# Strassen's scheme for the gate and up projections of a two-layer diffusion trunk

## The chip, the cores and the metric

The kernel runs on the 8 cores of one Trainium2 chip. All cores run the same program: core i takes two of the 16 context sequences and one of the 8 latent grids. The metric is the device time of the slowest core in microseconds (us). Some executions were slower, with a lower granted clock on one die (cores 0 to 3, or cores 4 to 7).

## The reference, cut to what matters

Two layers, each a mixer and then a SwiGLU channel mixer; every sub-layer is normalised, scaled and shifted ("modulated"), and added through a gate.

```python
D_MODEL, D_FF = 1024, 2816
def swiglu(h, wg, wu, wd):
    return (jax.nn.silu(h @ wg) * (h @ wu)) @ wd

for i in range(DEPTH):                      # DEPTH = 2
    ...                                     # layer 0: pooling + attention; layer 1: chunk_gmlp
    ctx = ctx + cg1 * y_ctx
    lat = lat + lg1 * y_lat
    h_ctx = rms_norm(ctx, norm_ffn_g[i]) * (1 + csc2) + csh2
    h_lat = rms_norm(lat, norm_ffn_g[i]) * (1 + lsc2) + lsh2
    ctx = ctx + cg2 * swiglu(h_ctx, ffn_wg[i], ffn_wu[i], ffn_wd[i])
    lat = lat + lg2 * swiglu(h_lat, ffn_wg[i], ffn_wu[i], ffn_wd[i])
```

A core has three blocks of 512 tokens: block 0 is context, blocks 1 and 2 are latents. In this document "first mixer" and "second mixer" are the SwiGLUs of the two layers, and "gated mixer" is the spatial-gating MLP (`chunk_gmlp`) between them.

## The kernel before

Everything is fused into one program. The kernel holds a planner of its own: each part (a normalisation, a projection, a stream of loads) is a generator that yields what it needs next, and the planner picks, by assumed durations, what to emit next and on which engine. The order on each engine is thus **fixed when the kernel is built** (in the traces, all eight cores show the same order on each engine, wherever no matmul record is missing); at run time only the times move. `RANK` and `T` are tuned constants of this planner. Matrices are stored with features on the partitions; `h[b]` has 8 tiles of 128 features x 512 tokens.

The SwiGLU, 256 hidden columns per `k`, 11 values of `k` in four groups `GR`:

```python
GR = [(0, 3), (3, 6), (6, 9), (9, 11)]
def up(gi):
    k0, k1 = GR[gi]
    for b in blocks:
        ...
        for k in range(k0, k1):
            wg, wu = wts[("g", k)], wts[("u", k)]
            for jj in range(2):
                js = slice(jj * 128, (jj + 1) * 128)
                ...                                   # the context of layer 0 uses a tanh form
                pg, pu = P.bank(), P.bank()           # two PSUM banks
                P.mmg(pg[:], [(wg[:, kc, js], hb[:, kc, :]) for kc in range(8)])
                P.mmg(pu[:], [(wu[:, kc, js], hb[:, kc, :]) for kc in range(8)])
                sg = P.tmp(F32)
                P.act(sg[:], pg[:], AF.Silu)                                # ScalarE
                P.tt("dve", a[:, 2 * (k - k0) + jj, :], pu[:], sg[:], ALU.mult)  # VectorE
def down(gi): ...                                     # the group's part of (..) @ wd, added to x
for gi in range(len(GR)):
    yield from up(gi)
    if gi > 0:
        yield from down(gi - 1)
yield from down(len(GR) - 1)
```

The last step of every normalisation, per 128 features (`xb` is the residual x, `rs` the reciprocal root mean square), and the one rule by which the planner reckons with VectorE and GpSimd working at the same time:

```python
P.stt("dve", tmp[:], xb[:, kc, :], AA[..., kc, ...], rs[:], ALU.mult, ALU.mult)   # x * scale * rs
P.affine(hb[:, kc, :], tmp[:], 1.0, mscal(l, sh, kc, b))                          # + shift; ScalarE, VectorE or GpSimd
...
if e == "dve" and not self.single and not any("/" in r[0] for r in rr + wr):      # "/": a PSUM operand
    d = max([d] + [z - start + d - 100.0 for a, z in self.pool_ops if a <= start < z])
```

So a VectorE operation with no PSUM operand is assumed to wait for a GpSimd operation that is under way. `stt` sets `self.single`, so the scalar_tensor_tensor form is exempt, and GpSimd is never assumed to wait.

## Time and profile before

The time before is 1142.12 us (median of 4 runs, 1141.41 to 1144.61).

| before | value | read from |
|---|---|---|
| TensorE busy | 1095.9 us, 96% | page, part 1 |
| VectorE / ScalarE / GpSimd busy | 62% / 34% / 15% | page, part 1 |
| chain that ended last | 81% TensorE | page, part 4 |
| TensorE busy, 460 to 640 us (first mixer) | 179.89 of 180 us | table of stretches |
| TensorE busy, 640 to 860 us (gated mixer and its surroundings) | 212.46 of 220 us | table of stretches |

These are lines of the page of the kernel before (busy us, share of the span, instructions; then busy tenths in 40 slices; then the chain by engine):

```profile
span 1141.4 us, 16800 instructions; the slowest of 8 cores (1139.3 to 1141.4 us)
PE 1095.9 (96%) x6155; PEld 510.4 (45%) x6155; DVE 707.7 (62%) x1234; ACT 389.6 (34%) x613; POOL 168.3 (15%) x263
PE   5799899899999999999999999999999999999998
DVE  1196899635767986568676999858631143134257
POOL 6141102010101131020011023204000010000000
PE 81%; DVE 10%; DMA 4%; issue 2%; ACT 2%; POOL 1%; DVEq 0%; ACTq 0%; POOLq 0%
```

The same core by stretches; the columns are in the header line:

```profile
core 7: us, PE busy (x) PEld busy (x) DVE busy (x) ACT busy (x) POOL busy (x), PEclk, DMA share, GB/s
220.00:380.00 160.00, 158.84 (x1421) 84.32 (x1420) 96.49 (x178) 114.40 (x120) 18.45 (x35) 1.00 0.82 172
460.00:640.00 180.00, 179.89 (x834) 81.43 (x833) 129.69 (x216) 25.95 (x41) 18.16 (x31) 1.00 0.78 157
640.00:860.00 220.00, 212.46 (x1048) 97.77 (x1047) 164.24 (x317) 84.75 (x166) 49.27 (x52) 1.00 0.29 49
860.00:1178.00 318.00, 278.26 (x1290) 125.82 (x1287) 105.30 (x144) 28.66 (x48) 7.38 (x14) 1.00 0.22 47
```

The reader is to see a TensorE without slack from about 240 us on, VectorE at 72% beside it in the first mixer (129.69 of 180), and a GpSimd that does little.

### The profile page before, as it was taken

How to read it: one execution, taken by the hardware profiler on the slowest of the kernel's cores; microseconds unless marked ns; L12 is line 12 of the kernel's file. 1: busy time of each engine (PE TensorE's matmuls, PEld its weight loads, DVE VectorE, ACT ScalarE, POOL GpSimd, SP SyncE). 2: the span in 40 equal slices, each digit the busy share in tenths (PEclk: the TensorE clock that was granted, in tenths of full speed). 3: DMA queues.
4: the chain of work that ended last, by engine and by line, in shares of the span. 5: the costliest groups of instructions: out<-in, count | busy, mean ns of one | idle time of the engine just before them, and what ended most of it. 6: DMA issues, size and time to landing. Idle time of an engine off the chain costs nothing.

```text
span 1141.4 us, 16800 instructions; the slowest of 8 cores (1139.3 to 1141.4 us)
## 1 busy us (share of the span) xinstructions
PE 1095.9 (96%) x6155; PEld 510.4 (45%) x6155; DVE 707.7 (62%) x1234; ACT 389.6 (34%) x613; POOL 168.3 (15%) x263
## 2 busy tenths in 40 slices
PE   5799899899999999999999999999999999999998
PEld 2344443454555444444444444444444444444443
DVE  1196899635767986568676999858631143134257
ACT  2155756778776231130101173342311101100100
POOL 6141102010101131020011023204000010000000
PEclk7699799799999999999999999999999999999999
DMA  9998837495997589865689600040942182030006
GB/s 177 170 254 147 138 99 128 76 161 121 235 217 179 124 131 171 178 116 105 157 177 194 146 1 1 1 74 9 161 71 37 25 142 37 1 56 1 1 1 221
DMA packets 38750, 126.74 MB, mean 111 GB/s; under 512 B 4832, under 2 KB 6752, under 8 KB 38672
## 3 DMA queue, kind: packets, MB, share of 16 engines
q0 software_dynamic: 25520, 91.41, 46.4%
q1 hardware_dynamic: 13152, 34.27, 9.3%
q8 instruction: 52, 0.85, 0.3%
q14 instruction: 26, 0.21, 0.1%
HBM read 194.91 MB, written 6.88 MB: 177 GB/s over the span
## 4 chain that ended last, share of the span: by engine, by line
PE 81%; DVE 10%; DMA 4%; issue 2%; ACT 2%; POOL 1%; DVEq 0%; ACTq 0%; POOLq 0%
PE pp L521 81%; DMA adaw_121<-ada_w 3%; DVE adaj_2991 L581 1%; DMA adaw_1322<-ada_w 1%; DVE tf_86 L573 0%; DVE tf_87 L561 0%; DVE tf_88 L573 0%; DVE tf_85 L573 0%; DVE tf_84 L573 0%; DVE tf_87 L573 0%; ACT L557 0%; DVE kT_2310 L617 0%; DVE tf_83 L573 0%; ACT tf_84 L557 0%; DVE qT_1673 L617 0%
## 5 line engine op out<-in xcount | busy, mean ns | idle before, releaser
L557 ACT ACTIVATE tf_87<-pp 128x512 f32<-128x512 f32 x25 | 14.9, 596 | 125.8 <-PE pp L521 115.3
L557 ACT ACTIVATE tf_83<-pp 128x512 f32<-128x512 f32 x22 | 13.1, 597 | 92.7 <-PE pp L521 92.7
L557 ACT ACTIVATE tf_85<-pp 128x512 f32<-128x512 f32 x23 | 13.7, 597 | 58.0 <-PE pp L521 44.0
L557 ACT ACTIVATE tf_86<-pp 128x512 f32<-128x512 f32 x26 | 15.5, 597 | 51.3 <-PE pp L521 51.2
L557 ACT ACTIVATE tf_84<-pp 128x512 f32<-128x512 f32 x21 | 12.5, 597 | 48.8 <-PE pp L521 48.7
L557 ACT ACTIVATE tf_88<-pp 128x512 f32<-128x512 f32 x21 | 12.5, 596 | 47.4 <-PE pp L521 47.4
L557 ACT ACT_TABLE_LOAD x17 | 21.8, 1283 | 8.6 <-PE pp L521 7.4
L561 DVE TENSOR_TENSOR mod_47<-pp,vecs_43 128x4 f32<-128x4 f32 x24 | 3.7, 159 | 29.8 <-PE pp L521 29.7
L521 PE MATMUL pp<-ones_46 128*128 128x512 bf16 x50 | 18.2, 518 | 1.5 <-DVE frac_54 L588 1.5
L573 DVE SCALAR_TENSOR_TENSOR x_3568<-pp,mod_47,x_3568 128x512 f32<-128x512 f32 x20 | 15.0, 750 | 7.2 <-PE pp L521 6.8
L573 DVE SCALAR_TENSOR_TENSOR x_4671<-pp,mod_47,x_4671 128x512 f32<-128x512 f32 x20 | 14.8, 747 | 6.3 <-PE pp L521 6.1
L573 DVE SCALAR_TENSOR_TENSOR x_4673<-pp,mod_47,x_4673 128x512 f32<-128x512 f32 x20 | 14.8, 747 | 5.8 <-PE pp L521 5.5
L573 DVE SCALAR_TENSOR_TENSOR x_4668<-pp,mod_47,x_4668 128x512 f32<-128x512 f32 x20 | 14.8, 747 | 5.0 <-PE pp L521 4.8
L573 DVE SCALAR_TENSOR_TENSOR x_3572<-pp,mod_47,x_3572 128x512 f32<-128x512 f32 x20 | 14.8, 748 | 4.6 <-PE pp L521 4.3
L573 DVE SCALAR_TENSOR_TENSOR x_3577<-pp,mod_47,x_3577 128x512 f32<-128x512 f32 x20 | 14.6, 746 | 4.1 <-PE pp L521 3.9
L573 DVE SCALAR_TENSOR_TENSOR x_3574<-pp,mod_47,x_3574 128x512 f32<-128x512 f32 x20 | 14.7, 747 | 3.8 <-PE pp L521 3.5
L573 DVE SCALAR_TENSOR_TENSOR x_4666<-pp,mod_47,x_4666 128x512 f32<-128x512 f32 x20 | 14.8, 747 | 3.6 <-PE pp L521 3.3
L573 DVE SCALAR_TENSOR_TENSOR x_1793<-pp,mod_47,x_1793 128x512 f32<-128x512 f32 x12 | 9.0, 748 | 3.5 <-PE pp L521 3.3
L573 DVE SCALAR_TENSOR_TENSOR x_1799<-pp,mod_47,x_1799 128x512 f32<-128x512 f32 x12 | 9.0, 747 | 3.5 <-PE pp L521 3.3
L573 DVE SCALAR_TENSOR_TENSOR x_1790<-pp,mod_47,x_1790 128x512 f32<-128x512 f32 x12 | 8.9, 749 | 3.5 <-PE pp L521 3.3
L573 DVE SCALAR_TENSOR_TENSOR x_1795<-pp,mod_47,x_1795 128x512 f32<-128x512 f32 x12 | 8.9, 747 | 3.5 <-PE pp L521 3.3
L557 ACT ACTIVATE tf_86<-x_3568 128x512 f32<-128x512 f32 x2 | 1.3, 630 | 28.6 <-DVE x_3568 L573 28.6
(2108 smaller groups left out, 2991.7 us busy)
## 6 DMA issues: line engine op xcount, KB each, us to landing
w_uq_142<-w_uq POOLq DMA_DIRECT2D x1, 576.0 KB, 55.4
x_93<-x_in POOLq DMA_DIRECT2D x1, 512.0 KB, 6.6
x_95<-x_in POOLq DMA_DIRECT2D x1, 512.0 KB, 7.3
x_97<-x_in POOLq DMA_DIRECT2D x1, 512.0 KB, 9.2
x_99<-x_in POOLq DMA_DIRECT2D x1, 512.0 KB, 10.0
adaw_107<-ada_w POOLq DMA_DIRECT2D x1, 512.0 KB, 20.0
adaw_109<-ada_w POOLq DMA_DIRECT2D x1, 512.0 KB, 22.6
adaw_111<-ada_w POOLq DMA_DIRECT2D x1, 512.0 KB, 24.7
```

Of the source, the lines that this page charges most:

```text
L521: ins = self.op("pe", lambda g: g.matmul(out, lhsT, rhs, start=start, stop=stop, **kw), [lhsT, rhs], [out], (c, 190), inc=inc)
L557: return self.op("act", lambda g: g.activation(out=out, in_=in_, func=func, bias=bias, scale=scale, **kw), reads, writes, d)
L561: return self.op(e, lambda g: g.tensor_tensor(out=out, in0=in0, in1=in1, op=op), [in0, in1], [out], self._d(e, out, [in0, in1], "tt"))
L573: ins = self.op(e, lambda g: g.scalar_tensor_tensor(out=out, in0=in0, scalar=sc, in1=in1, op0=op0, op1=op1), reads, [out], self._d(e, out, ...
L581: return self.op(e, lambda g: g.scalar_tensor_tensor(out=out, in0=in0, scalar=1.0, in1=in1, op0=ALU.mult, op1=ALU.mult, accum_out=acc), [i ...
```

## The change

Intent: gate and up tile of 128 hidden columns, times two halves of tokens, times two halves of the 1024 features, make a 2x2 block product of 8 block products. Strassen's scheme needs seven, so TensorE does 28 matmuls for 32, and sums of weights, sums of tokens and sums of results go to the other engines. It is used for latents in both layers (the halves are blocks 1 and 2) and for the context in the second (the halves are 256 tokens each). The first layer's context part stays plain.

```diff
+            def quad(p, k, jj, a):                    # cut: names of the blocks, yields
+                P.grow(v(E), P1)
+                P.copy(v(x1), v(E), engs=cp)          # cp = ("act",)
+                P.grow(v(F), P2)
+                P.tt("dve", v(x1), v(F), v(x1), ALU.add)
+                P.grow(v(C), P5)
+                P.copy(v(x3), v(C), engs=cp)
+                P.grow(v(E), P6, False)
+                P.copy(v(x2), v(E), engs=cp)
+                P.grow(v(C), P3, False)
+                P.tt("dve", v(x2), v(C), v(x2), ALU.add)
+                P.grow(v(E), P7, False)
+                P.copy(v(x4), v(E), engs=cp)
+                P.add2(v(x3), v(x3), v(x4), ALU.add)  # add2, mul: VectorE or GpSimd, as the planner picks
+                P.act(v(x3), v(x3), AF.Silu)
+                P.grow(v(E), P4, False)
+                P.act(v(x4), v(E), AF.Silu)
+                P.mul(a[b2][:, j, o2:o2 + n], v(x2), v(x3))
+                P.mul(a[b1][:, j, o1:o1 + n], v(x1), v(x4))
+            def wsum(k):                              # per 256 hidden columns
+                P.add2(s1[:], a21, a22, ALU.add)
+                P.add2(a21, a11, a21, ALU.subtract)   # in place: wg's tile is used up
+                P.add2(s2[:], s1[:], a11, ALU.subtract)
+                P.add2(s4[:], a12, s2[:], ALU.subtract)
+            def token_sums(p):                        # once per mixer and pair of halves, all on VectorE
+                yield U("dve", cond=has(...))         # both halves' normalised blocks must be there
+                for out, p_, q_ in ((T1[:], b12, b11), (T2[:], b22, T1[:]), (b12, b22, b12), (T4[:], b21, T2[:])):
+                    P.tt("dve", out, p_, q_, ALU.subtract)
```

With it came three things that are not the scheme: a new path in all normalisations,

```diff
-                P.stt("dve", tmp[:], xb[:, kc, :], AA[:, l, w, kc, ci:ci + 1], rs[:], ALU.mult, ALU.mult)
-                P.affine(hb[:, kc, :], tmp[:], 1.0, mscal(l, sh, kc, b))
+                xk, ak = xb[:, kc, :], AA[:, l, w, kc, ci:ci + 1]
+                if P.pick2(("dve", "pool"), "tt", tmp[:], [xk, rs[:]]) == "pool":
+                    P.tt("pool", tmp[:], xk, rs[:], ALU.mult)
+                    P.affine(hb[:, kc, :], tmp[:], ak, mscal(l, sh, kc, b), engs=("act", "dve"))
+                else:
+                    P.stt("dve", tmp[:], xk, ak, rs[:], ALU.mult, ALU.mult)
+                    P.affine(hb[:, kc, :], tmp[:], 1.0, mscal(l, sh, kc, b))
```

a reordered gated mixer (all `v` tiles before all `u` tiles, and its products `gT`, before all on GpSimd, may go to either engine: 23 of 24 go to VectorE), and re-tuned constants (32 values of `RANK` and `T`; the limit of weight tiles loaded ahead went from 13 to 8; filler matmuls from 50 to 79).

## The prediction

> **What bounds the kernel now.** TensorE. The page gives it 1095.9 us busy of 1141.4 (96%), and the chain of waits is 81% TensorE. Read by stage (table of stretches): in the second-layer channel mixer (840 us to the end) and in the first-layer one for latents (400 to 640 us) TensorE is busy 99%, granted clock 1.00, 187 matmuls of 512 columns per 40 us, so 214 ns each. Idle and cold clock lie before 240 us (about 32 us idle; clock 0.74 to 0.87 in some stretches) and around the gated mixer (640 to 840 us, 7.5 us idle). In the two mixers VectorE is busy 172 of 240 us and 109 of 301 us, ScalarE 41 and 32.
>
> **What changes.** The first mixer's context part (tanh form) stays plain. For latents in both layers, and context in the second, each pair of 128-column gate and up tiles with two token halves takes 28 matmuls for 32. Latents: 2 layers x 22 x 4 matmuls x 214 ns = 37.7 us less. Context: 28 of 256 columns for 16 of 512; at 107 ns each (half of 214) 3.0 us for 3.4, 22 times = 9.4 us less. Together 47 us of TensorE work. [...]
>
> Added, per latent quad (6.0 us of TensorE): ScalarE 4 evictions and 2 SiLU for 2 SiLU, at 596 ns: 3.6 us for 1.2; VectorE 2 sums from PSUM at 0.70 us, and an add and two products shared with GpSimd[...]. Weight sums: 4 per 256 columns[...], 88 in all; 12 token sums. Counting emitted operations with these durations, VectorE rises to about 88% over the latent part of the first mixer, where the second layer's modulation dots (1238 ns each) already run, and to about 60% in the second, where ScalarE is about 65%.
>
> [...]
>
> **How much is on the critical path.** All 47 us, since TensorE has no slack there. Given back, by my estimates: 3 us early (the re-tuned order emits 79 filler matmuls for 50: it expects to wait around 155 us, where before it had work; against it, the late modulation weight and cold clock around 195 to 210 us may go); 5 us in the first mixer from late sums on VectorE; 3 us in the second from ScalarE's in-order chain (the SiLU waits for a VectorE or GpSimd add, and evictions queue behind it); 2 us where the second mixer starts (weight and token sums first). Sum 13 us: 1142 - 47 + 13 = 1108 us.
>
> **What would show it.** TensorE busy falls by about 40 us; its waits on `tf`, `ws` and `ts` tiles between 400 and 600 us total under 8 us; 256-column matmuls pace at 107 to 110 ns; granted clock stays 1.00 in both mixers; second mixer from first product to end about 28 us shorter, first (latents) about 15 us.
>
> **What would make it wrong.** VectorE saturated in the first mixer, so that PSUM banks return late (10 to 20 us more); shallower weight prefetch (8 tiles for 13) stalling on DMA, whose share is 0.81 there; 256-column matmuls bound by weight loads (97 ns mean record) and slower than 110 ns; ScalarE chain limiting context quads; or a better early order, which would give more than 47.
>
> Chances: faster by over 2% 0.80, within 2% 0.17, slower 0.03. Predicted 1108 us, 1094 to 1127.

(3 + 5 + 3 + 2 gives the 13 us and 1142 - 47 + 13 the 1108. Measured in the two kernels, medians: an add or product of 512 columns 0.68 to 0.69 us on VectorE alone and 1.15 to 1.28 on GpSimd undisturbed, a weight sum 0.68 to 0.69 on VectorE alone and 2.1 to 2.5 on GpSimd, a dot 1.22, a sum from PSUM 0.69. The four terms are guesses of stage losses, not worked out from the trace. ScalarE's chain, the third, is in the changed kernel's trace: in the second mixer, 860 to 1178 us, its activations wait 20.9 us for VectorE's `tf` and 15.7 for GpSimd's.)

## More of the kernel before

(In the last stretch, the second mixer, this kernel ends at 1141 us. Of GpSimd's busy time in the page, 101 us are the issuing of 178 DMAs; its additions and products take 66 us.)

## The result, and the profile after

The changed kernel took **1179.62 us** (median of 4 runs; the three fast ones 1178.27 to 1180.26, one slow at 1296.77), against 1142.12 before. The ratio is 1.0317, 95% interval 1.0297 to 1.0338: slower by 3.2%. All ratios here are the mean time of a kernel's fast runs over that of the other's fast runs of the same rounds, so not quite the ratio of the medians quoted. Executions in which one die ran at a lower clock are left out of the means.

The page of the changed kernel, the same lines:

```profile
span 1177.9 us, 17956 instructions; the slowest of 8 cores (1167.7 to 1177.9 us)
PE 1076.6 (91%) x6272; PEld 522.2 (44%) x6272; DVE 882.0 (75%) x1406; ACT 520.2 (44%) x912; POOL 354.0 (30%) x390
PE   6799898899889988998999889996699999999998
DVE  1286889528677999999898999889865676575557
POOL 6151110100101082562353763306533430330200
PE 53%; DVE 24%; DMA 10%; issue 6%; POOL 4%; ACT 2%; another core or an unknown queue 0%; POOLq 0%; DVEq 0%; ACTq 0%; SPq 0%
```

and the same stretches:

```profile
core 2: us, PE busy (x) PEld busy (x) DVE busy (x) ACT busy (x) POOL busy (x), PEclk, DMA share, GB/s
220.00:380.00 160.00, 145.10 (x1349) 76.68 (x1349) 95.90 (x180) 116.88 (x121) 15.29 (x29) 0.97 0.88 185
460.00:640.00 180.00, 170.21 (x772) 75.37 (x771) 165.26 (x226) 72.06 (x130) 79.08 (x69) 0.98 0.53 121
640.00:860.00 220.00, 189.17 (x928) 87.96 (x927) 197.80 (x329) 82.58 (x172) 100.19 (x79) 0.94 0.32 57
860.00:1178.00 318.00, 309.43 (x1692) 163.48 (x1689) 198.82 (x290) 114.22 (x253) 74.54 (x79) 1.00 0.28 62
```

VectorE is now at 92% in the first mixer (165.26 of 180) and 90% around the gated mixer, GpSimd at 44 to 46%, and TensorE stands still for 10 and 31 us there. The chain that ended last is only 53% TensorE. In the waits, what TensorE waits for is mostly VectorE (total us, times, longest us):

```profile
PE pp L524 <- DVE x L582: 27.7, 17, 5.3
PE pp L524 <- DMA adaw<-ada_w: 13.8, 10, 5.0
PE pp L524 <- DVE gT L570: 8.9, 1, 8.9
PE pp L524 <- DVE tf L582: 7.5, 8, 2.4
PE pp L524 <- ACT tf L628: 7.2, 4, 4.8
```

(`x` is the residual: its addition reads a PSUM bank, so a late one means a PSUM bank that comes free late.) TensorE's own work did shrink as planned. In the second mixer matmuls of 512 columns start every 216 ns in both kernels, and those of 256 columns, which only the changed kernel has there, every 109 ns (medians; the means of back-to-back starts are 215.8 and 109.1). Summing all useful matmuls at these paces (two narrow forms at my estimates of 34 and 27 ns, close to the means of their starts before, 34.9 and 26.6; the medians are 29 and 25, and either cancels in the difference) gives 1047.9 us before and 1001.2 us after: 46.7 us less, as predicted.

So the loss is elsewhere. Take as "lost time" the time elapsed minus TensorE's pure matmul time up to there. Its growth by stage, from my alignment of the trace with the kernel's emitted order on the slowest core whose records are complete; the planner's own figures are beside it:

| lost in stage, us | plan before | chip before | plan after | chip after |
|---|---|---|---|---|
| up to the start of the latents' attention | 71 | 73.5 | 68 | 70.0 |
| that attention, with what fills it | 12 | 4.8 | 24 | 32.3 |
| from there to the first mixer's latents | 0 | 2.0 | 0 | 6.0 |
| first mixer (latents) | 1 | 0.9 | 3 | 20.3 |
| gated mixer and border to the second mixer | 6 | 6.8 | 10 | 28.2 |
| second mixer | 2 | 2.0 | 9 | 16.1 |
| sum | 92 | 90.0 | 114 | 172.9 |

Two facts stand in this table. The plan itself, computed when the kernel is built, gives back 22 of the 47 us (114 - 92): it ends at 1115.8 us, for 1140.3 before. And the chip, which kept within 3 us of the plan before (last matmul at 1138.3), ends 58.7 us behind it now (1174.5). 83 us are given back in all.

What the chip does that the plan does not know is in the timeline. VectorE from 702 us on, in the gated mixer (start us, us, instruction, count):

```profile
702.82 3.77 DVE L576 TENSOR_SCALAR h<-tf,AA,mod 128x512 bf16<-128x512 f32 x6
707.65 4.39 DVE L576 TENSOR_SCALAR h<-tf,AA,mod 128x512 bf16<-128x512 f32 x3
714.26 1.44 DVE L576 TENSOR_SCALAR h<-tf,AA,mod 128x512 bf16<-128x512 f32 x3
```

and GpSimd in the same stretch, the normalisation's new products back to back:

```profile
701.62 1.26 POOL L570 TENSOR_TENSOR tf<-x,tf 128x512 f32<-128x512 f32 x1
704.87 9.52 POOL L570 TENSOR_TENSOR tf<-x,tf 128x512 f32<-128x512 f32 x7 [1.99 <-ACT tf L566]
718.14 1.28 POOL L570 TENSOR_TENSOR tf<-x,tf 128x512 f32<-128x512 f32 x1 [3.74 <-DVE gT L570]
```

Three of VectorE's operations take 1.44 us where GpSimd is idle (its last product ends at 714.39), and 4.39 us while it works. Over the whole trace I split VectorE's operations by whether a GpSimd compute instruction overlaps them (medians, ns). The plan's figure is the time for which an operation keeps the engine; the planner has the result ready 80 ns later, so its 604 is to be compared with a recorded 684:

| VectorE operation in the changed kernel | plan | alone | beside GpSimd |
|---|---|---|---|
| normalisation, `h` (tensor_scalar, SBUF to SBUF) | 347 | 533 | 1376 (up to 3860) |
| normalisation, `tf`, two SBUF inputs (58 squares and sums; 17 scalar_tensor_tensor, 744 alone and 1753 beside) | 604 (624) | 692 | 1410 |
| weight sum `ws`, 1024 bf16 | 604 | 684 | 1214 (up to 3191) |
| product `a`, 512 columns | 604 | 676 | 1102 |
| `ssq` of the gated mixer, one element per partition | 71 | 158 | 1033 |
| sum from PSUM in a quad, 512 columns | 624 | 678 | 692 |
| residual from PSUM, `x` | 664 | 748 | 739 |

In this table only the operations without a PSUM operand are slowed, to 1.6 times (`a`) up to 6.5 times (`ssq`) their length alone; the last two rows, which read PSUM, change by 14 ns or less. By what mechanism, the traces do not show. But that a collision is visible does not say what it costs: an engine with slack can wait for nothing. That needs experiments.

### The profile page after: what moved, and what is told of

The parts are those of the page before. It is cut to its first block, busy times and chain, and to the rows that moved or that the text cites. A ratio compares the mean times of both kernels' runs of the same rounds, so it can differ in the third digit from the quotient of the medians.

```text
span 1177.9 us, 17956 instructions; the slowest of 8 cores (1167.7 to 1177.9 us)
## 1 busy us (share of the span) xinstructions
PE 1076.6 (91%) x6272; PEld 522.2 (44%) x6272; DVE 882.0 (75%) x1406; ACT 520.2 (44%) x912; POOL 354.0 (30%) x390
## 4 chain that ended last, share of the span: by engine, by line
PE 53%; DVE 24%; DMA 10%; issue 6%; POOL 4%; ACT 2%; another core or an unknown queue 0%; POOLq 0%; DVEq 0%; ACTq 0%; SPq 0%
PE pp L524 53%; DMA adaw<-ada_w 7%; DVE adaj L590 4%; DMA adat<-ada_t 4%; DVE x L582 3%; DVE tf L582 3%; DVE tf L570 3%; DVE h L576 3%; POOL tf L570 2%; DVE gT L570 1%; DVE a L570 1%; DVE ws L570 1%; DVE kT L629 1%; ACT tf L566 1%; POOL a L570 1%
## 5 line engine op out<-in xcount | busy, mean ns | idle before, releaser
L524 PE MATMUL pp<-a,wd 128*128 128x512 bf16 x1056 | 240.0, 384 | 22.8 <-DVE x L582 22.5
L628 ACT COPY tf<-pp 128x512 f32<-128x512 f32 (+1 forms) x267 | 134.8, 512 | 193.3 <-PE pp L524 183.3
L582 DVE SCALAR_TENSOR_TENSOR x<-pp,mod,x 128x512 f32<-128x512 f32 x208 | 151.6, 746 | 44.9 <-PE pp L524 42.0
L524 PEld LDWEIGHTS pp<-a,wd 128*128 128x128 bf16 x1056 | 103.0, 99 | 152.9 <-issue 36.9
L524 PE MATMUL pp<-h,wu 128*128 128x512 bf16 (+1 forms) x704 | 148.4, 354 | 2.0 <-DVE a L570 1.3
L590 DVE SCALAR_TENSOR_TENSOR adaj<-adat,cond 128x1024 bf16<-128x1024 f32 x96 | 129.8, 1353 | 20.1 <-DMA adat<-ada_t 18.4
L570 POOL TENSOR_TENSOR a<-tf,tf 128x512 bf16<-128x512 f32 (+1 forms) x66 | 80.3, 1219 | 166.9 <-ACT tf L566 161.8
L524 PE MATMUL pp<-ts,ws 128*128 128x512 bf16 (+1 forms) x528 | 116.8, 346 | 2.4 <-DVE ws L570 1.9
L566 ACT ACTIVATE pt<-pp,ksc 128x1024 bf16<-128x1024 f32 x96 | 102.2, 1111 | 28.7 <-PE pp L524 26.9
L524 PE MATMUL pp<-h,wg 128*128 128x512 bf16 (+1 forms) x440 | 101.3, 361 | 4.6 <-DVE tf L582 2.6
L566 ACT ACTIVATE tf<-x 128x512 f32<-128x512 f32 x45 | 28.2, 630 | 90.1 <-DVE x L582 89.7
L566 ACT ACTIVATE tf<-pp 128x512 f32<-128x512 f32 (+1 forms) x94 | 51.6, 549 | 22.7 <-PE pp L524 20.9
```

The costliest lines, as they stand in the source:

```text
L524: ins = self.op("pe", lambda g: g.matmul(out, lhsT, rhs, start=start, stop=stop, **kw), [lhsT, rhs], [out], (c, 190), inc=inc)
L566: return self.op("act", lambda g: g.activation(out=out, in_=in_, func=func, bias=bias, scale=scale, **kw), reads, writes, d)
L570: return self.op(e, lambda g: g.tensor_tensor(out=out, in0=in0, in1=in1, op=op), [in0, in1], [out], self._d(e, out, [in0, in1], "tt"))
L582: ins = self.op(e, lambda g: g.scalar_tensor_tensor(out=out, in0=in0, scalar=sc, in1=in1, op0=op0, op1=op1), reads, [out], self._d(e, out, ...
L590: return self.op(e, lambda g: g.scalar_tensor_tensor(out=out, in0=in0, scalar=1.0, in1=in1, op0=ALU.mult, op1=ALU.mult, accum_out=acc), [i ...
L628: return self.op("act", lambda g: g.copy(out=out, in_=in_), [in_], [out], durs[e])
```

## The experiments

Fifteen kernels ran. Those named s_ keep the changed kernel's (in s_second: c_second's) exact instruction order and semaphores, with the planner's accounting untouched, and let some emitted instructions work on 8 columns; their results are wrong, and the readers of tiles left unwritten read other, valid data. The core of the edit, the same in all with another condition:

```diff
+    def few(self, *aps):
+        return [bass.AP(a.tensor, a.offset, [list(a.ap[0]), [a.ap[-1][0], 8]]) for a in aps]
     def tt(self, e, out, in0, in1, op):
-        return self.op(e, lambda g: g.tensor_tensor(out=out, in0=in0, in1=in1, op=op), [in0, in1], [out],
+        o, a, b = self.few(out, in0, in1) if self.small(e, out, [in0, in1]) else (out, in0, in1)
+        return self.op(e, lambda g: g.tensor_tensor(out=o, in0=a, in1=b, op=op), [in0, in1], [out],
```

The theory was that VectorE and GpSimd hold each other up, so that VectorE, nearly full, returns PSUM banks and tiles late. Rivals: VectorE simply has too much to do; late loads of the modulation weights at the head of VectorE's queue; GpSimd's results come late in any case; the re-tuned order itself.

### Which work costs: s_new, s_vec, s_pool, s_dotdma

```diff
 # s_new   small(): the scheme's sums and products (weight sums, token sums, quad adds and products), VectorE and GpSimd
 # s_vec   small(): the same, VectorE's alone
 # s_pool  small(): GpSimd's adds and products in both mixers and in the normalisations, not its weight sums
 # s_dotdma: the modulation dots on 8 columns, and their loads bring 64 of 1024 columns:
+            o = bass.AP(out.tensor, out.offset, [list(out.ap[0]), [1, 64]])
+            i = bass.AP(in_.tensor, in_.offset, [list(in_.ap[0]), [1, 64]])
```

> The changed kernel with every instruction in its exact order; the added sums and products of the new scheme on VectorE and GpSimd (weight sums, token sums, adds, products) work on 8 columns, so they cost next to nothing; results wrong on purpose. Theory A (the added element-wise work overloads VectorE and returns banks late): most of the loss after 455 us goes, time 1120 to 1140 us. Rival B (the re-tuned order itself loses, whatever the added work costs): time above 1160 us.

> As s_new, but only VectorE's part of the added sums and products works on 8 columns; GpSimd's part stays whole. Theory A: at least half of what s_new gains. If collisions with GpSimd are the larger half, the remaining VectorE work is still slowed and less than half is gained.

> As the changed kernel in exact order, but GpSimd's products and adds of the mixers and of the normalisations work on 8 columns; VectorE keeps all its work. Theory A in its form of collisions: [...]the time falls by over 20 us, below 1158. In its form of plain load: less than 10 us gained.

> The changed kernel in exact order, but the modulation dots of the second layer work on 8 columns and their loads bring 64 of 1024 columns; results wrong on purpose. Rival B (dots placed where their loads come late hold up VectorE's queue during attention, 240 to 400 us): the stretch from 220 to 455 us gets some 15 to 20 us shorter. Theory A adds a gain after 455 us, since VectorE loses 50 to 60 us of other work there: total 1130 to 1150 us. If neither, above 1165.

(Measured means at 512 columns, changed kernel and s_pool: `tf` with two SBUF inputs 763 and 688 ns, `a` 986 and 793.)

Measured, with before at 1143.2 us: s_new 1155.05 (ratio 1.0100), s_vec 1162.04 (1.0163), s_pool **1138.45** (0.9957, interval 0.9911 to 1.0002), s_dotdma 1164.78 (1.0187). Against 1.0317 of the changed kernel, these are gains of about 25, 18, 41 and 15 us; the intervals leave each uncertain by 3 to 6 us. s_new falls between its two ranges: the added work explains part of the loss, not most of it. s_vec and s_pool fall where the theory has them; s_dotdma ends at the edge of "neither", and the stretch up to 455 us is 9 us shorter for 15 to 20 expected.

The shortened GpSimd operations of s_pool gain more than all of the scheme's sums in s_new, though VectorE keeps all its own work. It is therefore not the amount of VectorE's work alone. With GpSimd out of the way VectorE's unchanged `h` operations take 541 ns (groups by form, busy us and mean ns):

```profile
L597 DVE TENSOR_SCALAR h<-tf,AA,mod 128x512 bf16<-128x512 f32 x41 | 21.0, 541 | 0.0
L591 DVE TENSOR_TENSOR ws<-wu,ws 128x1024 bf16<-128x1024 bf16 x21 | 14.5, 692 | 0.8
```

where the changed kernel has

```profile
L576 DVE TENSOR_SCALAR h<-tf,AA,mod 128x512 bf16<-128x512 f32 x41 | 36.8, 924 | 1.2 <-POOL tf L570 1.2
L570 DVE TENSOR_TENSOR ws<-wu,ws 128x1024 bf16<-128x1024 bf16 x21 | 21.9, 1041 | 0.8
```

Lost time by stage (as in the table above) falls from 20.3 to 3.3 in the first mixer, from 28.2 to 14.8 around the gated mixer, and from 16.1 to 10.3 in the second; the attention stage stays at 33.1. s_dotdma shows the other piece. VectorE waits for loads of modulation weights (`adat`) between 200 and 400 us, in the changed kernel and in s_dotdma:

```profile
DVE adaj L590 <- DMA adat<-ada_t: 18.4, 9, 4.8
DVE adaj L615 <- DMA adat<-ada_t: 1.4, 2, 0.9
```

The attention stage's lost time falls by 7 us, to 24.9, which is within 1 us of the plan's 24; another 7 us are gained in the first mixer (13.2 lost, for 20.3). The run shortens the dots on VectorE together with their loads, and with these the traffic for all other loads, so it does not tell which of the three counts.

### Which part of GpSimd's work: s_xn, s_qp

```diff
 # s_xn: small() = only the normalisations' products on GpSimd
 # s_qp: small() = only the two mixers' adds and products on GpSimd
```

> The changed kernel in exact order; only the normalisations' products on GpSimd (64 of 512 columns, a path that the change added) work on 8 columns; results wrong on purpose. If this path is the larger part of what s_pool gained (41 us): time 1150 to 1160, and the gain lies at the borders of the stages (before the gated mixer's products and in it). If the block products' own GpSimd work is the larger part: above 1165.

> The counterpart of s_xn: only GpSimd's adds and products of the two mixers work on 8 columns. If they are the larger part of s_pool's gain: 1145 to 1160, with the gain between 455 and 692 us. Otherwise above 1165. s_xn and s_qp together should make up the 41 us of s_pool if the two parts do not depend on each other.

s_xn took 1148.13 us (ratio 1.0057, interval 1.0034 to 1.0080), a gain of about 30; s_qp had one fast run, 1163.65 us beside 1141.85, a gain of about 14 (two further runs were slow, so there is no ratio). The two gains add up to s_pool's 41 within the noise. Most of what s_pool gains is thus bought by the normalisations' work on GpSimd, which has nothing to do with Strassen: of the 64 operations that s_xn shortens, 55 are products of the new path, which the kernel before does not have, and nine are squares and sums, of which it has 17. In s_xn the first mixer still loses 14.8 us, and in s_pool, with the mixers' products shortened too, 3.3.

### Late results or SBUF traffic: s_lat, s_lat2

A shortened operation also ends earlier, so its readers start earlier. s_lat and s_lat2 put tiny fills in front of the shortened operation, so that the result comes as late as the full one, without its traffic.

```diff
 # s_lat and s_lat2: s_pool, and
+            pads = [bass.AP(out.tensor, out.offset + 8 * st * (i + 1), [list(out.ap[0]), [st, 8]])
+                    for i in range(n_fills)]          # s_lat: 8 or 4; s_lat2: 22 (512 columns) or 10 (256)
+            for p in pads:
+                g.memset(p, 0.0)
```

> As s_pool, but each shortened GpSimd operation is preceded by a row of tiny fills, so that it ends about as late as the full one (1.1 to 1.3 us) while it reads and writes only a few columns. [...] If what costs is that VectorE's and ScalarE's queues wait for GpSimd's late results: back above 1165.

> The changed kernel in its exact order, with the GpSimd adds and products of both gated mixers and of the normalisations reduced to 8 columns (as in s_pool, 1138.5 us), but now behind 22 (10 for 256 columns) tiny fills on GpSimd, so that the result comes after about 1.0 to 1.3 us, as late as the full operation alone on its engine (1.16 us). s_lat was the same with too few fills. Results wrong on purpose. Theory A (what costs is that the full operations and VectorE's hold each other up while both read and write on-chip memory): the time stays near s_pool, 1136 to 1146 us. Rival (the results of GpSimd simply come later than VectorE's would, whoever else works): most of the 41 us comes back, 1160 us or more.

(In these expectations "mixers" are the two SwiGLUs. The sentence cut from the first named a mechanism that no run shows; its range, if GpSimd's traffic is what slows VectorE, was near s_pool and below 1148 us.) s_lat took 1140.06 us (ratio 0.9987, interval 0.9965 to 1.0008), but its fills were too short to decide: eight fills and the operation last 0.50 us. In s_lat2 22 fills and the operation last 1.08 us (median of 129), near the 1.15 to 1.28 us of a full operation that nothing disturbs. It ran on another chip, on which cores 4 to 7 had a lower clock in every run, of before too (0.958 against 0.974), so I compare the slowest core of the undisturbed die, median over the runs: 1136.7 us for s_lat2 beside 1140.7 us for before, ratio 0.9965 (s_pool, on its own chip in the same way: 1137.35 beside 1141.9, 0.9960). Nothing of the 41 us comes back beyond the noise. That GpSimd's results come late in any case is ruled out as their cause; it is the two engines' use of SBUF at the same time.

### Do the two pieces add: s_pd

```diff
 # s_pool's condition, and s_dotdma's shortened dots and loads, in one kernel
```

> s_pool and s_dotdma together: the GpSimd adds and products and also the modulation dots and their loads shortened, exact order of the changed kernel, results wrong on purpose. If the two losses are separate (loads that come late ahead of the first mixer; collisions from the first mixer's normalisations on), their gains add: 1138.5 less 9 to 15, so 1123 to 1130 us. If the dots' gain is only time that the collisions free as well: 1136 to 1140 us.

On the same chip as s_lat2; the slowest core of the undisturbed die is 1125.7 us beside 1140.7, ratio 0.987 (five runs; in a sixth both dies were slow). That is 11 us below s_lat2 and s_pool (0.9965, 0.9960), within the 9 to 15 expected, so the gains add. With both gone the kernel is 15 us faster than before; of the 47 us, some 32 are still given back. Of these the plan itself gives back 22. For the rest, s_pd has its last matmul 7 us behind its plan (1122.9 for 1115.8), where the kernel before is 2 us ahead of its own (1138.3 for 1140.3).

### The scheme alone, in the second mixer: c_second, s_second

The kernel before, its order and constants, with the scheme in the second mixer only (correct results), and the same with GpSimd's weight sums shortened.

```diff
 # c_second, against the changed kernel (and with before's constants, gated mixer and normalisations):
+            new = t in F["S"]                         # F["S"] = "b": the second mixer
             def up(gi):
-                if tanh:
+                if not new:
                     yield from plain(gi)
                     return
 # s_second, against c_second:
+        return self.nfree(out) >= 256 and (e == "pool" and nm in ("ws", "wg"))    # small()
```

> The kernel before, with its own order and constants, and the new scheme in the second mixer only (instruction for instruction the kernel before up to about 740 us). There 28 us of matrix work go and VectorE has room. Theory A with the GpSimd path as culprit: 1120 to 1136 us, a clear gain over before; the loss at the start of the second mixer (weight and token sums) 5 to 12 us. If the scheme itself cannot pay (ScalarE's chain, 256-column matmuls): 1138 or more.

> The kernel before with the scheme in the second mixer only (as c_second, 1141.5 us beside 1141.9 for before), in its exact order, with the weight sums that GpSimd does reduced to 8 columns; results wrong on purpose. c_second loses 18 us at the border between the gated mixer and the second mixer and 8 inside the second mixer. If these are collisions of GpSimd's weight sums with VectorE's squares: 10 us or more of it come back, ratio 0.991 or less. If they come from the order itself (the second mixer no longer starts while the gated mixer still runs, because the token sums need whole normalised blocks): ratio 0.996 to 1.001.

c_second took 1141.49 us beside 1141.85, ratio 1.0007 (0.9989 to 1.0025): 28 us of matrix work removed, all given back. It loses 25.4 us at the border (6.8 before) and 10.6 us inside (2.0). At the border the trace shows VectorE's squares for the normalisation, whose length alone is 0.69 us:

```profile
788.45 2.21 DVE L595 TENSOR_TENSOR tf<-x 128x512 f32<-128x512 f32 x1
791.42 1.76 DVE L595 TENSOR_TENSOR tf<-x 128x512 f32<-128x512 f32 x1
793.22 2.49 DVE L595 TENSOR_TENSOR tf<-tf,tf 128x512 f32<-128x512 f32 x1
```

while GpSimd, in the same kernel, does weight sums without a pause:

```profile
787.92 2.17 POOL L595 TENSOR_TENSOR ws<-wg 128x1024 bf16<-128x1024 bf16 x1
790.18 2.46 POOL L595 TENSOR_TENSOR wg<-wu,wg 128x1024 bf16<-128x1024 bf16 x1
792.60 2.56 POOL L595 TENSOR_TENSOR ws<-ws,wu 128x1024 bf16<-128x1024 bf16 x1
```

That picture is persuasive, and it is less than a third of the matter. s_second took 1136.83 us, ratio 0.9937 (0.9923 to 0.9950), between what the two theories expected: some 8 us come back. The other 20 us are not these collisions; they stand in the plan already, which ends at 1132.4 for 1140.3 before, so with 8 of the 28 us: it loses 12 us more than before's plan at the border, and 8 inside the second mixer. Before, the second mixer starts at 764.9 us, while the gated mixer still works on later blocks until 807.6 us, and fills its gaps. By the scheme it starts at 810.5 us, after the gated mixer's end: token sums need whole normalised halves, and the first quads wait for them. That is the 12 us at the border; what makes the 8 inside was not tested.

### A plan that avoids overlaps, for the whole change: r_port

A full, correct kernel. The planner is to let no two SBUF operations of VectorE and GpSimd overlap; weight sums are on VectorE, constants searched anew (2250 plans).

```diff
-        if e == "dve" and not self.single and not any("/" in r[0] for r in rr + wr):
-            d = max([d] + [z - start + d - 100.0 for a, z in self.pool_ops if a <= start < z])
-        elif e == "pool":
-            self.pool_ops = self.pool_ops[-3:] + [(start, start + d)]
+        if e in self.port and d > 150.0 and not any("/" in r[0] for r in rr + wr):
+            for a, z in sorted(self.port["pool" if e == "dve" else "dve"]):
+                if a <= start < z:
+                    start = z
+            self.port[e] = self.port[e][-12:] + [(start, start + d)]
...
-                P.add2(s1[:], a21, a22, ALU.add)
+                P.tt("dve", s1[:], a21, a22, ALU.add)
```

> A full, correct kernel: the scheme in both mixers as in the changed kernel, but the planner, which fixes every engine's order at build, lets no VectorE and GpSimd operation on on-chip memory run at the same time (PSUM operands excepted), all weight sums are on VectorE, and the start and rank constants were searched again under that rule. Its plan ends at 1118.5 us. Theory A (collisions that the old planner did not count explain most of the 58 us by which the chip fell behind the old plan of 1115.8): the chip ends within 15 us of the plan, 1120 to 1134 us, below both kernels. Rival (the plan is missed for other reasons, such as late loads and the tight order): 1150 to 1180 us.

1175.57 us beside 1157.88 us on the chip with the slow die; by the slowest core of the undisturbed die 1164.2 beside 1140.7, 2.1% slower where the changed kernel is 3.2% slower. The time is in the rival's range: the plan ends at 1118.5, and a core of that die has its last matmul at 1157.3, 39 us late. The collisions are still there (`h` takes 535 ns alone and 1376 beside GpSimd, 22 of 54 times).

But the edit does not do what the expectation says. It moves an operation only if its planned start falls inside one that is planned already; a GpSimd operation that is emitted later, starts before such a VectorE operation and runs into it, stays. Rebuilding the plan from kernel.py gives 82 such overlaps among its 549 VectorE operations on SBUF (by the same count 190 of 556 in the changed kernel), and 31 of the 54 `h` are among them. So r_port tests a plan with fewer collisions, not one without. That engines also drift away from a plan, which fixes their order and not the time, may add to it; no run tests that. The trace has the extreme case, one `h` operation on VectorE (0.49 us alone),

```profile
413.44 5.71 DVE L578 TENSOR_SCALAR h<-tf,mod 128x512 bf16<-128x512 f32 x1
```

that starts while GpSimd issues DMAs and ends only after four GpSimd products which started after it:

```profile
412.26 1.66 POOL L443 DMA_DIRECT2D wd<-ffn_wd  x3
413.92 4.94 POOL L572 TENSOR_TENSOR tf<-x,tf 128x512 f32<-128x512 f32 x4
```

### A version built on the cause: r_late, r_late2, r_both

If the second mixer's gain goes into the lost overlap and into collisions while VectorE is short of time, keep both away. In the cut below the kernel's flags are spelled out. r_late is the kernel before, with its constants; the second mixer's first group (3 of 11 `k`) is computed plainly, block by block, so that it can still start inside the gated mixer; its down projection follows at once and covers the sums; the scheme takes over from `k` = 3; weight sums are on VectorE. The normalisations are as before.

```diff
             for gi in range(len(GR)):
-                yield from up(gi)
-                if gi > 0:
-                    yield from down(gi - 1)
+                yield from up(gi)                     # second mixer: plain for gi == 0, quads after
+                if gi == 0 and t == "b":
+                    for p in halves:
+                        P.spawn(RANK["ts" + t], token_sums(p), "ts" + t)
+                    yield from down(0)
+                elif gi > 0 and not (gi == 1 and t == "b"):
+                    yield from down(gi - 1)
```

r_late2 also takes the quads' adds and products off GpSimd; r_both does what r_late does in both mixers, with the planner free to use GpSimd for weight sums too. Both have constants searched anew.

> A full, correct kernel: the one before, with the scheme only for chunks 3 to 10 of the second mixer. Its first three chunks are computed plainly (all 16 products), block by block, so that they can start while the gated mixer still works on later blocks, as before; their down projection comes right after them and covers the sums; weight sums are all on VectorE; constants as before. The scheme then saves 8/11 of its 23.5 us there, 17 us of TensorE. The plan ends at 1124.0 (before: 1140.3). Theory (what the second mixer's gain went into is the lost overlap and GpSimd's collisions): ratio 0.984 to 0.991, below both kernels. Rival (any use of the scheme in the second mixer is given back to VectorE's added work): ratio 0.996 to 1.003.

> As r_late, with nothing of the second mixer on GpSimd (all sums and products on VectorE) and the rank and start constants searched again; plan 1121.8 us. Nothing of the second mixer can collide with GpSimd here, so if collisions matter inside it, it is as fast as r_late or faster by up to 4 us: ratio 0.982 to 0.990. If a fuller VectorE costs more than collisions: 2 to 6 us slower than r_late.

> As r_late but with the scheme for chunks 3 to 10 of both mixers, first three chunks plain in both, the planner free to use GpSimd for sums and products, normalisations as before (no GpSimd product added), constants searched again; plan 1117.8 us. If the normalisations' GpSimd products and the lost overlap are the main causes, the chip stays within 10 us of the plan: ratio 0.979 to 0.988. If the weight sums and products on GpSimd in the first mixer collide as in the changed kernel, it falls 15 to 25 us behind the plan: ratio 0.992 to 1.001.

r_late took **1125.00 us** (1124.35 to 1126.42, all five) beside 1143.91, ratio **0.9836** (0.9822 to 0.9849): faster than both kernels (1.6%, clear of the noise), with correct results, and 3.3 us ahead of its plan of 1124.0 (last matmul at 1120.7). Its page:

```profile
span 1123.9 us, 17495 instructions; the slowest of 8 cores (1121.4 to 1123.9 us)
PE 1078.7 (96%) x6283; PEld 522.1 (46%) x6283; DVE 773.8 (69%) x1349; ACT 447.8 (40%) x757; POOL 207.3 (18%) x300
```

and the table of its stretches:

```profile
460.00:640.00 180.00, 179.89 (x834) 81.43 (x833) 129.52 (x215) 26.11 (x41) 18.16 (x31) 1.00 0.78 156
640.00:860.00 220.00, 212.44 (x1049) 97.79 (x1047) 164.41 (x318) 84.95 (x166) 47.16 (x48) 1.00 0.22 38
860.00:1120.00 260.00, 260.00 (x1419) 137.36 (x1418) 170.54 (x259) 86.06 (x192) 49.29 (x55) 1.00 0.31 64
```

TensorE is busy all 260.00 us of the last stretch. The collisions are not gone: VectorE's products `a` there still take 1125 ns on average (676 alone in the changed kernel). They cost nothing, because VectorE is at 66% (170.54 of 260) and TensorE waits for nothing there (no wait from 850 to 1122 us). The scheme keeps most of what it saves: TensorE's matmuls sum to 1027.7 us for 1047.9, 20.2 us less (8/11 of the 27.7 us that the whole second mixer saves at these paces; the 23.5 in my expectation was a slip, half of 47, forgetting that only the second mixer treats the context too), lost time grows by 2.6 us, and the time falls by 18.9. Its three differences from c_second (the plain first group, the order of its down projection, weight sums on VectorE) were not tried one by one.

r_late2 took 1135.37 us, ratio 0.9923 (0.9906 to 0.9941), above its expectation and 6.8 us behind its plan (last matmul 1128.6, plan 1121.8). Taking the last GpSimd work away makes nothing faster there; since its constants differ as well, how much a fuller VectorE and how much the new order costs is not told apart. r_both took 1141.57 us, ratio 0.9979 (0.9967 to 0.9990), the rival's range: 20 us behind its plan at the last matmul. It loses 20 us more than before already ahead of the latents' attention, where no part of the scheme runs (12 of them stand in its own plan, by its new constants), and 5 us in the first mixer. So the scheme in the first mixer was not made to pay, but this run does not show that it cannot.

## Why the prediction was wrong

The predicted time was 1108 us, 1094 to 1127; it is 1179.62.

1. "TensorE bounds the kernel" and "47 us of TensorE work less" were right: 46.7 us by the same paces, matmuls of 256 columns at 109 ns, half the 216 of 512 columns, so not slowed by their weight loads (98 ns, median record).
2. "All 47 us on the critical path, since TensorE has no slack there" was right of the kernel before. It does not carry over: the change made VectorE the pace-setter, 92% and 90% busy in the stretches where it counts.
3. The step that failed is **"Given back, by my estimates ... Sum 13 us"**. The measure is 83 us: 28 in the attention stage, 4 at the first mixer's start, 19 in it, 21 around the gated mixer and 14 in the second mixer, less 3 at the start. The prediction had 3 for the early order, 5 for the first mixer, 3 for the second, 2 for its start.
4. The cause that it undersized, VectorE's operations slowed beside GpSimd's, was named in it. But it sized this on the kernel before, where collisions are rare: 40 of 479 VectorE operations on SBUF overlap a GpSimd operation, for 184 of 631 in the changed kernel. It put the surcharge on additions at a quarter, from figures that the trace does not show. 46 such operations average 711 ns, and 688 where no GpSimd operation runs; beside GpSimd the time about doubles (691 to 1342 ns in the changed kernel). The runs put the collisions at 41 us (s_pool, with s_lat2 against the rival), 30 of them from the normalisations' work on GpSimd (s_xn), which the prediction did not list among what the change adds.
5. "VectorE saturated in the first mixer ... 10 to 20 us more" stood as a risk, and happened; it was the right mechanism in the wrong column. The two stages after it, which the prediction costed at 5 us together, lost another 35.
6. The early order was costed at 3 us and loses 28 in the attention stage. 7 to 9 us of it go when the modulation dots and their loads are shortened (s_dotdma; s_pd beside s_pool), where dots waited for their loads at the head of VectorE's queue; 12 us the plan itself gives away there. The other 7 or so are what the kernel before ran ahead of its own plan in this stage (4.8 us lost for 12 planned), and why it did is open.
7. Of what should show it: TensorE busy fell by 19 us (1095.9 to 1076.6), not 40, probably since slower matmuls after pauses and the 29 more fillers count as busy too (after a pause of 5.3 us that ended at 543.8 us the next matmuls of 512 columns started 427 ns apart for 5.9 us, then 216 again; granted clock 0.83 from 540 to 560 us); waits on `tf`, `ws`, `ts` were indeed small in the first mixer (1.9 us), because the late VectorE shows at `x`, which holds the PSUM banks (12.3 us): the wrong tiles were named. The clock stayed at 0.98 and 1.00 in the two mixers; around the gated mixer it fell to 0.94.
8. The kernel's own plan, which is computed at build and needs no chip, ended only 24.5 us earlier than before's. So it shows 22 us given back for the prediction's 13, and would have corrected that sum by 9 of the missing 70 us, had I read it. The rest is what the plan does not know.

What is shown: collisions cost about 41 us; they act through SBUF traffic and not through late results; the modulation dots with their loads cost about 11 to 15; in the second mixer alone the order costs more (20, of which 12 at the border with its lost overlap) than GpSimd's weight sums (8); a version that changes both keeps the gain. Not shown: which of load and dot counts, and what a plan really free of overlaps would do, since r_port's is not. Open: some 7 us of the attention stage, and a profitable scheme in the first mixer.

## What to carry to other kernels

Work taken off the bounding engine is worth its time only if the engines that receive it keep slack where that engine waits; compute their load per stage with durations *beside each other*, not alone. Moving elementwise work from VectorE to GpSimd was no relief here while VectorE had SBUF operations to do at the same time (s_xn: about 30 us gained without it). An addition or product of 512 columns took 1.15 to 1.28 us on GpSimd for 0.68 to 0.69 on VectorE, and such an operation on VectorE beside it about 1.1 to 1.4 (`a`, `tf`): look at the same VectorE operation with and without GpSimd under way before believing in it. And a rewrite that needs whole blocks first (sums over tokens) destroys overlap at its border; a plain first part that keeps the overlap and covers the sums, with the weight sums off GpSimd, turned a tie (1.0007) into 1.6% here.
